# A second layout of x and an earlier row norm chain in layer 0, and another home for the gathered rows of the expert pairs

## The chip, the cores and the metric

The program runs on one core of one Trainium2 chip. TensorE (PE), VectorE (DVE), ScalarE (ACT) and GpSimd (POOL) each work through an instruction stream of their own, in order. SyncE (SP) issues most of the DMAs. The metric is the device time of one execution in microseconds (us), as the median of several runs. All arithmetic is in float32; many matmuls take operands split in a high and a low part (dtype float32r), three products to one.

## The reference

Two layers of an encoder on 512 tokens of width 1024:

```python
for l in range(DEPTH):                       # DEPTH = 2
    h = rmsnorm(x, attn_norm_g[l])
    x = x + hybrid_mixer(h, ...)             # h @ W_in (1024 x 2464), 16 attention heads, @ W_out
    h = rmsnorm(x, ffn_norm_g[l])
    x = x + expert_choice_ffn(h, ...)        # 16 experts, each takes its 64 best tokens
return rmsnorm(x, final_norm_g)

# expert_choice_ffn, for each expert e:
gate, idx = top_k(affinity[:, e], 64)
xe = h[idx]                                  # 64 x 1024
y  = (silu(xe @ w_gate[e]) * (xe @ w_up[e])) @ w_down[e]     # 1024 x 1408, 1024 x 1408, 1408 x 1024
out[idx] += y * gate
```

The rotary angles of the attention heads come from `positions`. The weights of the experts are some 277 MB for each layer; everything else is small beside that.

## The kernel before, in words

**Projection.** `attention` computes h @ W_in with the tokens along the matmul's columns (feature-major): `xh` and `xl` hold the high and the low part of x transposed and multiplied by the norm's gain, 8 row blocks k of 128 features by 512 tokens. The norm's factor per token is applied later: `row_norms` (L350) squares and sums x's rows on ACT (L354) and a power on POOL (L178) gives `rstd`, which `spread` (L360, PE at L364) turns into a row `rb`. The columns of W_in come in chunks. `split(i)` makes a chunk's weights into a high part (ACT, L332) and the rest (DVE, L333). PE then does 24 matmuls for a chunk (L733: 8 blocks k, three products). `spread` stands in PE's order behind the second chunk.

**x transposed.** `turn_x(t)` (L336) has PE transpose 8 blocks of 128 tokens (L342), DVE multiply them out of PSUM by the gain (`gx`, L346), ACT make the high part (L347) and DVE the rest (L348). `heat` (L368) puts matmuls on the identity in between, `START` says how many. This runs in both layers.

**Angles.** In layer 0 `make_angles` computes the rotary angles by some 45 small DVE instructions on 128x128 tiles (L212 to L231), pumped out ahead of the first chunk's matmuls; their sines go to ACT (L241), and `make_tables` (L246) spreads them by PE behind the third chunk.

**Experts.** They are worked through in 8 pairs. A pair takes 24 weight loads of 1408 KB: 8 row blocks of w_gate, 8 of w_up, 8 of w_down. `load` (L153) issues each on SP, into the buffer that `extra` names: `SEQ` for the first 16 loads of a layer, after that the list `again` round and round, 14 buffers. `x0` to `x11` are tiles of the expert pool, `s0` to `s2` of the ring that also holds W_in. A load can be issued when PE has done the matmuls on what lay in its buffer. The gathered rows of a pair's 128 tokens (indirect DMA from `xrow_d`, L1162, scaled on ACT, L1163) have buffer x0, which the first load of the layer has used. `turn_rows` (L1165) transposes them for PE. For the first pair the rows' first half is made by PE from x itself (`fill`, L1136), the second half comes from the gather.

**What sets the order.** Each engine's order is fixed when the program is built: a recording layer puts instructions in an order by its own priorities, except where `keep_in_program_order` pins one. A buffer of a pool is handed out again when its last reader is done.

**End of layer 0.** `put` (L1266) adds the last pair's results: for 6 of the 8 half blocks of x, PE has already put x itself into PSUM, and the sum is copied back (L1281) by ACT or DVE as `END_ON` says; the other two are added by DVE (L1279).

Of the kernel before, what the change touches and what calls it, by code (L numbers as in the profile page):

```python
# [11 lines left out]
F32 = mybir.dt.float32  # L12
# [119 lines left out]
def body(ctx, tc, x_in, pos, w_in, w_uq, w_ukv, w_out, w_gate, w_up, w_down, gatt, gfin, params, consts, band, sel, out):  # L132
# [53 lines left out]
    def make_angles(pool):  # L186
# [9 lines left out]
        for t in range(NT):  # L196
            nc.sync.dma_start(pi[32 * t : 32 * t + 32], pos[:, t * P : (t + 1) * P].to_broadcast([32, P]))
# [60 lines left out]
    def attention(l, ap, wk, op):  # L258
# [19 lines left out]
        xh = op.tile([P, KD, S], F32R, tag="big", name="xh")  # L278
        xl = [wk.tile([P, 4, S], F32R, tag="st", bufs=4, name=nm("xl")) for _ in range(2)]
# [19 lines left out]
        def fetch():  # L299
            if len(loaded) < len(plan):  # L300
# [13 lines left out]
        steps, sines = make_angles(wk) if l == 0 else (iter(()), None)  # L314
        nc.sync.dma_start(pg, params[l])
# [7 lines left out]
        def split(i):  # L323
# [13 lines left out]
        def turn_x(t):  # L337

            for h in range(2):
                pt = bank()  # L340
                for k in range(4):
                    nc.tensor.transpose(pt[:, k * P : (k + 1) * P], x[:, t, (h * 4 + k) * P : (h * 4 + k + 1) * P], ident)  # L342
                gx = wk.tile([P, S], F32, tag="P", bufs=PB, name=nm("gx")).rearrange("p (k s) -> p k s", k=4)
                g = gcol[:, l, h * 4 : h * 4 + 4].unsqueeze(2).to_broadcast([P, 4, P])
                hv = xh[:, h * 4 : h * 4 + 4, t * P : (t + 1) * P]
                nc.vector.tensor_tensor(gx, pt.rearrange("p (k s) -> p k s", k=4), g, op=ALU.mult)  # L346
                nc.scalar.copy(hv, gx)  # L347
# [1048 lines left out]
```

## Time and profile before

| what | us |
|---|---|
| median of 3 runs | 1937.29 (1937.24 to 1938.94) |
| the profiled execution, its own time | 1935.57 |
| its span | 1933.8 |
| PE busy | 1729.4 (89%) |
| DVE busy | 709.3 (37%) |
| ACT busy | 429.0 (22%) |
| bytes moved by DMA | 647.75 MB, mean 335 GB/s |

The span is the time from the first to the last instruction; 1.8 us of the execution's own time lie around it. A busy share of 89% for PE is a mean over stages with different limits, so it doesn't yet say what bounds the kernel. The chain of waits has DMA on 51% of the span and PE on 35%.

### The profile page before, as it was taken

Reading aid. Unit: us, or ns where it says so; the run is one execution under the profiler, and the core shown is the slowest. Engines: PE = TensorE matmul, PEld = TensorE weight load, DVE = VectorE, ACT = ScalarE, POOL = GpSimd, SP = SyncE. Lnnn points to the kernel's source line nnn. Section 1 sums busy time; section 2 is a strip of 40 time slices with the busy share of each in tenths; the row PEclk is TensorE's granted clock in tenths of the full one; section 3 lists DMA queues with packets and bytes.
Section 4 is the critical chain, followed back from the end, with each engine's and each line's share of the span. In section 5 each row is a group of like instructions: output and inputs, shape, how many; then the busy total and the mean of one; then the engine's idle time right before and its main releaser. Section 6 shows DMA issues by size and latency. Waiting matters only on the chain.

```text
span 1933.8 us, 22166 instructions
## 1 busy us (share of the span) xinstructions
PE 1729.4 (89%) x8838; PEld 888.7 (46%) x8838; DVE 709.3 (37%) x1481; ACT 429.0 (22%) x883; POOL 205.6 (11%) x232
## 2 busy tenths in 40 slices
PE   7999999999887888878889999989998888888786
PEld 6786676444332333323377856754443333323223
DVE  6877866211211112111178698551221112111112
ACT  4337952101000100000043489311100100001001
POOL 1314421000000000000013253110000000000000
PEclk9999999999999999999999999999999999999999
DMA  6765648899999999999938735689999999999996
GB/s 223 205 186 85 163 151 337 352 423 425 425 424 424 424 425 425 425 423 425 403 116 262 158 82 126 227 318 418 424 425 424 424 425 424 424 424 425 425 425 252
DMA packets 102758, 647.75 MB, mean 335 GB/s; under 512 B 11040, under 2 KB 28192, under 8 KB 53504
## 3 DMA queue, kind: packets, MB, share of 16 engines
q1 hardware_dynamic: 88336, 606.34, 77.9%
q0 software_dynamic: 12256, 36.07, 7.9%
q10 hardware_dynamic: 2064, 3.93, 0.6%
q8 instruction: 69, 1.13, 0.2%
q14 instruction: 33, 0.27, 0.0%
HBM read 617.60 MB, written 27.39 MB: 334 GB/s over the span
## 4 chain that ended last, share of the span: by engine, by line
DMA 51%; PE 35%; DVE 9%; ACT 3%; issue 1%; POOL 1%; SPq 0%; DVEq 0%; ACTq 0%; POOLq 0%
DMA xslot<-in_w_up_dram 12%; DMA xslot<-in_w_gate_dram 11%; DMA xslot<-in_w_down_dram 10%; PE ps L1215 7%; PE ps L733 6%; DMA slot<-in_w_up_dram 6%; DMA slot<-in_w_gate_dram 6%; DMA slot<-in_w_down_dram 6%; PE ps L834 4%; PE ps L1255 4%; PE ps L742 2%; PE ps L651 2%; PE ps L634 2%; DVE sm L583 1%; PE ps L494 1%
## 5 line engine op out<-in xcount | busy, mean ns | idle before, releaser
L1215 PE MATMUL ps<-xslot,xe 128*64 128x506 f32 (+1 forms) x2400 | 511.0, 566 | 80.1 <-DMA xslot<-in_w_up_dram 57.4
L1215 PEld LDWEIGHTS ps<-xslot,xe 128*64 128x64 f32 x2400 | 162.0, 137 | 410.7 <-issue 260.2
L1255 PE MATMUL ps<-xslot,hx 128*64 128x512 f32 (+3 forms) x1392 | 252.6, 507 | 35.6 <-DMA xslot<-in_w_down_dram 31.0
L1234 DVE TENSOR_TENSOR hx<-ps,hx 128x506 f32<-128x506 f32 (+1 forms) x48 | 43.5, 970 | 453.4 <-PE ps L1215 453.4
L1255 PEld LDWEIGHTS ps<-xslot,hx 128*64 128x64 f32 x1392 | 92.8, 137 | 186.1 <-issue 119.4
L1182 ACT ACTIVATE hx<-ps,gates 128x512 fp32r<-128x512 f32 x32 | 20.3, 684 | 676.2 <-PE ps L1255 676.2
L1215 PE MATMUL ps<-slot,xe 128*64 128x506 f32 (+1 forms) x648 | 140.4, 568 | 21.0 <-DMA slot<-in_w_up_dram 15.1
L1183 DVE SCALAR_TENSOR_TENSOR hx<-ps,gates,hx 128x512 fp32r<-128x512 f32 x32 | 22.5, 746 | 366.2 <-ACT hx L1182 366.2
L733 PE MATMUL ps<-xh,w 128*128 128x512 f32 (+1 forms) x448 | 146.0, 409 | 12.1 <-ACT xh L347 12.1
L1193 DVE TENSOR_TENSOR x<-ps,x 128x512 f32<-128x512 f32 x112 | 69.5, 683 | 172.5 <-PE ps L1191 172.5
L590 ACT ACTIVATE P<-ps,sm 128x512 f32<-128x512 f32 x168 | 116.6, 704 | 32.0 <-DVE sm L583 30.8
L1162 POOL DMA_INDIRECT xslot<-xrow_d,slots x16 | 15.3, 959 | 961.2 <-DVE oh L1155 942.2
L1163 ACT ACTIVATE xslot<-xslot,slots 128x1024 f32<-128x1024 f32 x16 | 18.4, 1148 | 442.9 <-DMA xslot<-xrow_d,slots 442.9
L733 PEld LDWEIGHTS ps<-xh,w 128*128 128x128 f32 (+1 forms) x448 | 85.7, 192 | 36.0 <-ACT xh L347 13.2
L1215 PEld LDWEIGHTS ps<-slot,xe 128*64 128x64 f32 x648 | 44.0, 137 | 110.8 <-issue 71.0
L733 PE MATMUL ps<-xl,w 128*128 128x512 f32 (+1 forms) x224 | 85.7, 393 | 0.0
L583 DVE TENSOR_REDUCE sm<-ps 128x1 f32<-128x512 f32 x120 | 78.7, 679 | 5.8 <-PE ps L568 4.8
L1255 PE MATMUL ps<-slot,hx 128*64 128x512 f32 (+3 forms) x400 | 71.7, 498 | 9.2 <-DMA slot<-in_w_down_dram 8.4
L634 PE MATMUL ps<-ident,P 128*128 128x128 f32 x512 | 77.8, 275 | 1.2 <-ACT P L590 1.1
L642 ACT COPY pt<-ps 128x512 f32<-128x512 f32 x118 | 68.9, 605 | 26.0 <-PE ps L634 25.8
L634 PEld LDWEIGHTS ps<-ident,P 128*128 128x128 f32 x512 | 62.6, 141 | 24.5 <-ACT P L590 7.0
L333 DVE TENSOR_TENSOR w<-slot,w 128x1024 fp32r<-128x1024 f32 (+4 forms) x46 | 53.8, 1171 | 30.2 <-ACT w L332 27.2
(280 smaller groups left out, 2119.9 us busy)
## 6 DMA issues: line engine op xcount, KB each, us to landing
xslot<-in_w_gate_dram SPq DMA_DIRECT2D x100, 1408.0 KB, 27.1
xslot<-in_w_up_dram SPq DMA_DIRECT2D x100, 1408.0 KB, 28.0
xslot<-in_w_down_dram SPq DMA_DIRECT2D x100, 1408.0 KB, 27.0
slot<-in_w_gate_dram SPq DMA_DIRECT2D x28, 1408.0 KB, 27.1
slot<-in_w_down_dram SPq DMA_DIRECT2D x28, 1408.0 KB, 27.0
slot<-in_w_up_dram SPq DMA_DIRECT2D x26, 1408.0 KB, 28.3
slot<-in_w_in_dram SPq DMA_DIRECT2D x8, 1536.0 KB, 7.3
st<-bst_d POOLq DMA_DIRECT2D x40, 256.0 KB, 4.4
```

Of the source, the lines that this page charges most:

```text
L333: nc.vector.tensor_tensor(w[:, 1, :, o : o + m], src, w[:, 0, :, o : o + m].bitcast(F32), op=ALU.subtract)
L583: nc.vector.tensor_reduce(mn, ps, axis=AX.X, op=ALU.min)
L590: nc.scalar.activation(e, ps, AF.Exp, bias=mn, scale=-1.0, accum_out=lcol)
L634: nc.tensor.transpose(b[:, kc * P : (kc + 1) * P], e[:, kc * P : (kc + 1) * P], ident)
L642: nc.scalar.copy(dv, bv)
L651: nc.tensor.matmul(o[64 * i : 64 * i + 64], heads[2 * m + i][4][:, kc, :], pts[i][:, kc, :], start=(kc == 0), stop=(kc == NT - 1))
L733: nc.tensor.matmul(b[:m], w[:, passes[j][0], k, :m], passes[j][1](k), start=(n == 0), stop=(n == 3 * KD - 1))
L834: nc.tensor.matmul(blocks[t][1 + h], o, w[h], start=(i == 0), stop=(i == 3 * KD - 1))
L1193: nc.vector.tensor_tensor(xv, b, xv, op=ALU.add)
L1215: tc.keep_in_program_order(nc.tensor.matmul(b[64 * i : 64 * i + 64, : qn * NJ], xe[:, k, 64 * i : 64 * i + 64], ws[i][:, q0 * NJ : (q0 + q ...
L1234: nc.vector.tensor_tensor(hv, u[:, : qn * NJ].rearrange("p (q j) -> p q j", j=NJ), hv, op=ALU.mult)
L1255: tc.keep_in_program_order(nc.tensor.matmul(bs[h][64 * i : 64 * i + 64, e % 512 : e % 512 + z - e], hT[:, j, 64 * i : 64 * i + 64], ws[i][ ...
```

## The change

In layer 0 a second copy of x, transposed (`x_t`), is loaded where x was, and the parts are made from it without PE; x itself is loaded later. The positions come ready for one DMA. The angles are pumped out ahead of the row norm, and all of `START` stands ahead of the first chunk. In layer 1 the transposes follow each other without a break, and the low parts are pinned behind all of them. In the experts, the first pair's rows are fetched as half rows into a third buffer of the tag `oh`; the other pairs' rows have x7, the buffer of the tenth load, in place of x0, and the second pair's are fetched later (`ROWS_AT`). `END_ON` is all ACT.

```diff
-START = [[6, 0, 2, 6, 4], [2, 0, 0, 4, 2]]
+START = [18, 2]
+ROWS_IN = 7
+ROWS_AT = 2
-END_ON = 'avavav'
+END_ON = 'aaaaaa'
...
-        for t in range(NT):
-            nc.sync.dma_start(pi[32 * t : 32 * t + 32], pos[:, t * P : (t + 1) * P].to_broadcast([32, P]))
+        nc.sync.dma_start(pi, pos)
...
+        xs = [wk.tile([P, 4, S], F32, tag="st", bufs=4, name=nm("xs")) for _ in range(2 if l == 0 else 0)]
...
                     if l == 0 and not loaded and a == 0:
-                        for t in range(NT):
-                            tc.keep_in_program_order(nc.sync.dma_start(x[:, t, :], x_in[t * P : (t + 1) * P, :]))
+                        for k in range(0, KD, 2):
+                            src = x_t[k * P : (k + 2) * P, :].rearrange("(k p) s -> p k s", p=P)
+                            tc.keep_in_program_order(nc.sync.dma_start(xs[k // 4][:, k % 4 : k % 4 + 2, :], src))
...
         steps, sines = make_angles(wk) if l == 0 else (iter(()), None)
+        if l == 0:
+            for t in range(NT):
+                tc.keep_in_program_order(nc.sync.dma_start(x[:, t, :], x_in[t * P : (t + 1) * P, :]))
...
-                nc.vector.tensor_tensor(w[:, 1, :, o : o + m], src, w[:, 0, :, o : o + m].bitcast(F32), op=ALU.subtract)
+                rest = lambda o=o, m=m, src=src: nc.vector.tensor_tensor(w[:, 1, :, o : o + m], src, w[:, 0, :, o : o + m].bitcast(F32), op=ALU.subtract)
+                if lower is None:
+                    rest()
+                else:
+                    lower.append(lambda rest=rest: tc.keep_in_program_order(rest()))
...
-                nc.vector.tensor_tensor(xl[h][:, :, t * P : (t + 1) * P], gx, hv.bitcast(F32), op=ALU.subtract)
+            return lambda: tc.keep_in_program_order(nc.vector.tensor_tensor(xl[h][:, :, t * P : (t + 1) * P], gx, hv.bitcast(F32), op=ALU.subtract))
+
+        def part_x(k):
+
+            g, xv = gcol[:, l, k : k + 1], xs[k // 4][:, k % 4, :]
+            nc.scalar.activation(xh[:, k, :], xv, AF.Copy, scale=g)
+            nc.vector.scalar_tensor_tensor(xl[k // 4][:, k % 4, :], xv, g, xh[:, k, :].bitcast(F32), op0=ALU.mult, op1=ALU.subtract)
...
-        if l > 0:
-            ready = split(0)
-        for t in range(NT):
-            heat(START[l][t])
-            turn_x(t)
+        heat(START[l])
         if l == 0:
             ready = split(0)
-        heat(START[l][NT])
+            for k in range(KD):
+                part_x(k)
+            pump(100)
+        else:
+            ready = split(0, lower := [])
+            rest = {(t, h): turn_x(t, h) for t in range(NT) for h in range(2)}
+            for fn in lower + [rest[t, h] for h in range(2) for t in range(NT)]:
+                fn()
         rstd = row_norms()
...
-        pump(100)
...
-                again = [q for q in SEQ if q not in (0, "hx")]
+                again = [q for q in SEQ if q not in (ROWS_IN, "hx")]
...
-            slots = fw.tile([P, 144], F32, tag="slots", bufs=1, name=nm("slots"))
-            info = slots[:, 0:128].rearrange("p (t g i) -> p t g i", t=NT, g=8)
+            slots = fw.tile([P, 16], F32, tag="slots", bufs=1, name=nm("slots"))
+            info = pg[:, 0:128].rearrange("p (t g i) -> p t g i", t=NT, g=8)
...
-                v = xslot(0)[:, :D]
-                nc.gpsimd.indirect_dma_start(v, None, xrow_d[l][:, :], bass.IndirectOffsetOnAxis(token[:, p : p + 1], 0))
+                if p > 0:
+                    v, src = xslot(ROWS_IN)[:, :D], xrow_d[l][:, :]
+                else:
+                    v, src = fw.tile([P, S], F32R, tag="oh", bufs=3, name=nm("rows")).bitcast(F32), xrow_d[l].rearrange("t (h d) -> (t h) d", h=2)
+                nc.gpsimd.indirect_dma_start(v, None, src, bass.IndirectOffsetOnAxis(token[:, p : p + 1], 0))
...
                         if w is w_gate and k == MARK_AT and p < 7:
                             ohs[p + 1] = marks(p + 1)
-                            rows = fetch_rows(p + 1)
+                            if p > 0:
+                                rows = fetch_rows(p + 1)
+                        if w is w_up and k == ROWS_AT and p == 0:
+                            rows = fetch_rows(1)
```

VectorE at the start of layer 0, before (`gx`, `xl`: parts of x; `w`: the second chunk's rest; `tabw`: angles):

```order
L346 TENSOR_TENSOR gx_283<-ps_278,gcol 128x512
L346 TENSOR_TENSOR gx_292<-ps_287,gcol 128x512
L213 CAST tabw_192<-tabw_192 128x128
L348 TENSOR_TENSOR xl_177<-gx_283,xh 128x4x128
L348 TENSOR_TENSOR xl_178<-gx_292,xh 128x4x128
L214 TENSOR_SCALAR tabw_192<-tabw_192,cn 128x128
L333 TENSOR_TENSOR w_380<-slot_179,w_380 128x1024
L215 TENSOR_SCALAR tabw_192<-tabw_192 128x128
```

VectorE at the same place now, from its first weights on:

```order
L339 TENSOR_TENSOR w_229<-slot_181,w_229 128x1024
L363 SCALAR_TENSOR_TENSOR xl_179<-xs_177,gcol,xh 128x512 x4
L363 SCALAR_TENSOR_TENSOR xl_180<-xs_178,gcol,xh 128x512 x4
L339 TENSOR_TENSOR w_324<-slot_181,w_324 128x1024
L214 CAST tabw_194<-tabw_194 128x128
L215 TENSOR_SCALAR tabw_194<-tabw_194,cn 128x128
L216 TENSOR_SCALAR tabw_194<-tabw_194 128x128
```

Eight products out of PSUM and the instructions around them are gone; two angle steps have moved behind the second chunk's rest.

VectorE a little later in layer 0 now, where the row norm's `v` stands, which before was the fifth of its rows:

```order
L210 TENSOR_SCALAR tabw_195<-tabw_195 128x128
L211 TENSOR_TENSOR tabw_195<-tabw_195 128x128
L372 TENSOR_SCALAR v_293<-ss_284 128x4
L231 COPY tabw_195<-tabw_195 128x128
L232 TENSOR_SCALAR tabw_195<-tabw_195 128x128
```

The step that leads to `rstd` has moved behind most of the angles.

VectorE at the start of layer 1, before, from the last sums of x on:

```order
L1279 TENSOR_TENSOR x<-ps_5766,x 128x512
L1279 TENSOR_TENSOR x<-ps_5770,x 128x512
L346 TENSOR_TENSOR gx_5883<-ps_5878,gcol 128x512
L346 TENSOR_TENSOR gx_5892<-ps_5887,gcol 128x512
L346 TENSOR_TENSOR gx_5901<-ps_5896,gcol 128x512
L348 TENSOR_TENSOR xl_5858<-gx_5883,xh 128x4x128
L346 TENSOR_TENSOR gx_5910<-ps_5905,gcol 128x512
L348 TENSOR_TENSOR xl_5859<-gx_5892,xh 128x4x128
L333 TENSOR_TENSOR w_5872<-slot_5860,w_5872 128x1024
L348 TENSOR_TENSOR xl_5858<-gx_5901,xh 128x4x128
L348 TENSOR_TENSOR xl_5859<-gx_5910,xh 128x4x128
L346 TENSOR_TENSOR gx_5919<-ps_5914,gcol 128x512
```

The same stretch now (five of the eight `gx`, then the rest of the first weights):

```order
L355 TENSOR_TENSOR gx_5850<-ps_5845,gcol 128x512
L355 TENSOR_TENSOR gx_5858<-ps_5853,gcol 128x512
L355 TENSOR_TENSOR gx_5866<-ps_5861,gcol 128x512
L355 TENSOR_TENSOR gx_5874<-ps_5869,gcol 128x512
L355 TENSOR_TENSOR gx_5882<-ps_5877,gcol 128x512
L339 TENSOR_TENSOR w_5819<-slot_5804,w_5819 128x1024
L357 TENSOR_TENSOR xl_5802<-gx_5826,xh 128x4x128
L357 TENSOR_TENSOR xl_5802<-gx_5842,xh 128x4x128
```

All eight `gx` stand ahead of every `xl` and of the weights' rest.

## Rows read from the trace of the kernel before

**Rows 1.** Windows: from:to, length, busy of each engine (count), PEclk, DMA share, GB/s.

```profile
8.00:10.00 2.00, 2.00 (x13) 2.00 (x12) 0.00 (x0) 1.54 (x4) 0.00 (x0) 1.00 1.03 418
...
21.70:26.70 5.00, 5.00 (x12) 3.94 (x13) 4.79 (x16) 0.54 (x1) 0.00 (x0) 0.50 0.80 265
...
41.20:125.00 83.80, 83.80 (x360) 63.40 (x359) 73.46 (x117) 26.60 (x41) 27.26 (x21) 1.00 0.69 210
...
337.00:345.60 8.60, 7.53 (x49) 4.40 (x46) 2.33 (x8) 0.00 (x0) 1.09 (x1) 1.00 0.23 98
...
357.00:435.00 78.00, 77.28 (x413) 31.67 (x413) 14.33 (x26) 6.32 (x7) 1.90 (x2) 1.00 1.01 423
...
1290.90:1297.70 6.80, 5.73 (x26) 2.70 (x26) 2.11 (x7) 0.00 (x0) 1.08 (x1) 0.75 0.22 63
```

**Rows 2.** Chain that ended last: start, length, what; one chunk, one steady load.

```profile
35.82 5.57 PE ps L733 x24
...
435.04 27.17 DMA xslot<-in_w_down_dram
```

**Rows 3.** Timeline, start of layer 0: start, length, instruction, count, idle before and releaser.

```profile
6.90 1.06 ACT L354 ACTIVATE junk<-x 128x1024 f32<-128x1024 f32 x1 [0.17 <-DMA x<-in_x_dram]
...
6.92 3.28 PE L342 MATMUL ps<-ident,x 128*128 128x128 f32 x16 [2.48 <-DMA x<-in_x_dram]
...
12.38 1.04 POOL L178 TENSOR_TENSOR r<-v,mhalf 128x4 f32<-128x4 f32 x1 [9.02 <-DVE v L357]
...
12.70 1.04 PE L342 MATMUL ps<-ident,x 128*128 128x128 f32 x8
...
13.30 1.05 ACT L332 CAST w<-slot 128x1024 fp32r<-128x1024 f32 x1 [1.21 <-DMA slot<-in_w_in_dram]
...
21.70 6.25 PE L733 MATMUL ps<-xh,w 128*128 128x512 f32 x16 [7.00 <-ACT xh L347]
...
23.08 1.22 DVE L333 TENSOR_TENSOR w<-slot,w 128x1024 fp32r<-128x1024 f32 x1
...
31.90 0.29 DVE L210 TENSOR_TENSOR tabw<-tabw 128x128 f32<-128x128 f32 x1
...
35.22 0.60 PE L364 MATMUL ps<-ident,r 128*128 128x128 f32 x4
```

**Rows 4.** Timeline, first expert pair of layer 0: weight loads, first steps, gather.

```profile
327.14 0.43 SPq L155 DMA_DIRECT2D slot<-in_w_up_dram  x1
...
335.82 2.58 PE L1215 MATMUL ps<-xslot,xe 128*64 128x506 f32 x12 [0.38 <-DVE xe L1139]
...
342.91 2.58 PE L1215 MATMUL ps<-xslot,xe 128*64 128x506 f32 x12
...
343.87 1.09 POOL L1162 DMA_INDIRECT xslot<-xrow_d,slots  x1 [9.52 <-PE ps L1150]
...
345.54 3.93 SPq L155 DMA_DIRECT2D xslot<-in_w_down_dram  x2
...
351.39 0.65 PE L1170 MATMUL ps<-ident,xslot 128*128 128x128 f32 x4
```

**Rows 5.** DMA issues at 327.14 and 378.35: count, KB, us to landing.

```profile
slot<-in_w_up_dram SPq DMA_DIRECT2D x1, 1408.0 KB, 13.8
...
xslot<-in_w_gate_dram SPq DMA_DIRECT2D x1, 1408.0 KB, 14.9
```

**Rows 6.** Timeline, start of layer 1.

```profile
969.61 1.87 DVE L346 TENSOR_TENSOR gx<-ps,gcol 128x512 f32<-128x512 f32 x3
...
975.79 1.88 DVE L346 TENSOR_TENSOR gx<-ps,gcol 128x512 f32<-128x512 f32 x3
...
978.37 1.96 PE L733 MATMUL ps<-xh,w 128*128 128x512 f32 x5 [4.70 <-ACT xh L347]
...
980.11 0.62 ACT L347 CAST xh<-gx 128x512 fp32r<-128x512 f32 x1 [1.79 <-DVE gx L346]
...
991.60 0.60 PE L364 MATMUL ps<-ident,r 128*128 128x128 f32 x4
```

More of the change, by code (lines that the diff above doesn't have):

```diff
@@ L131, in body @@
 @with_exitstack
-def body(ctx, tc, x_in, pos, w_in, w_uq, w_ukv, w_out, w_gate, w_up, w_down, gatt, gfin, params, consts, band, sel, out):
+def body(ctx, tc, x_in, x_t, pos, w_in, w_uq, w_ukv, w_out, w_gate, w_up, w_down, gatt, gfin, params, consts, band, sel, out):
     nc = tc.nc
@@ L321, in attention, with split @@
         fetch()
-        def split(i):
+        def split(i, lower=None):
             gi, cols, ks = chunks[i]
@@ L332, in split, with turn_x @@
                 nc.scalar.copy(w[:, 0, :, o : o + m], src)
-                nc.vector.tensor_tensor(w[:, 1, :, o : o + m], src, w[:, 0, :, o : o + m].bitcast(F32), op=ALU.subtract)
+                rest = lambda o=o, m=m, src=src: nc.vector.tensor_tensor(w[:, 1, :, o : o + m], src, w[:, 0, :, o : o + m].bitcast(F32), op=ALU.subtract)
[3 more added lines that the diff above has]
+                    lower.append(lambda rest=rest: tc.keep_in_program_order(rest()))
                 o += m
             return w, o
[L337 to L347, printed above, removed]
-                nc.vector.tensor_tensor(xl[h][:, :, t * P : (t + 1) * P], gx, hv.bitcast(F32), op=ALU.subtract)
+        def turn_x(t, h):
+            pt = bank()
+            for k in range(4):
+                nc.tensor.transpose(pt[:, k * P : (k + 1) * P], x[:, t, (h * 4 + k) * P : (h * 4 + k + 1) * P], ident)
+            gx = wk.tile([P, S], F32, tag="P", bufs=PB, name=nm("gx")).rearrange("p (k s) -> p k s", k=4)
+            g = gcol[:, l, h * 4 : h * 4 + 4].unsqueeze(2).to_broadcast([P, 4, P])
+            hv = xh[:, h * 4 : h * 4 + 4, t * P : (t + 1) * P]
+            nc.vector.tensor_tensor(gx, pt.rearrange("p (k s) -> p k s", k=4), g, op=ALU.mult)
+            nc.scalar.copy(hv, gx)
+            return lambda: tc.keep_in_program_order(nc.vector.tensor_tensor(xl[h][:, :, t * P : (t + 1) * P], gx, hv.bitcast(F32), op=ALU.subtract))
[3 more added lines that the diff above has]
+            nc.vector.scalar_tensor_tensor(xl[k // 4][:, k % 4, :], xv, g, xh[:, k, :].bitcast(F32), op0=ALU.mult, op1=ALU.subtract)
         def row_norms():
@@ L1098, in body @@
             state["extra"] = extra
-            slots = fw.tile([P, 144], F32, tag="slots", bufs=1, name=nm("slots"))
-            info = slots[:, 0:128].rearrange("p (t g i) -> p t g i", t=NT, g=8)
-            token, scales = slots[:, 128:136].bitcast(I32), slots[:, 136:144]
+            slots = fw.tile([P, 16], F32, tag="slots", bufs=1, name=nm("slots"))
+            info = pg[:, 0:128].rearrange("p (t g i) -> p t g i", t=NT, g=8)
+            token, scales = slots[:, 0:8].bitcast(I32), slots[:, 8:16]
             nc.gpsimd.tensor_copy(info[:, :, :, 0:2], a_all.rearrange("p t (g i) -> p t g i", i=2))
@@ L1222, in body @@
                             if k == HALF_AT:
-                                turn_rows(rows, xe, 4)
+                                turn_rows(rows, xe, 4, 4)
                         if w is w_gate and k in SCATTER_AT and pending is not None:
@@ L1347, in shape_constants @@
     return consts, band, np.tile(sel.reshape(32, 6 * P), (4, 1))
-_INS = ["x", "positions", "w_in", "mla_w_uq", "mla_w_ukv", "w_out", "w_gate", "w_up", "w_down", "gatt", "gfin", "params", "consts", "band", "sel"]
+_INS = ["x", "x_t", "positions", "w_in", "mla_w_uq", "mla_w_ukv", "w_out", "w_gate", "w_up", "w_down", "gatt", "gfin", "params", "consts", "band", "sel"]
 def lay_out(inputs):
@@ L1359, in lay_out @@
     got["x"] = a["x"].reshape(S, D)
-    got["positions"] = a["positions"].reshape(1, S)
+    got["x_t"] = np.ascontiguousarray(got["x"].T)
+    got["positions"] = np.repeat(a["positions"].reshape(NT, P), 32, axis=0)
     got["gatt"] = np.ascontiguousarray(a["attn_norm_g"].reshape(L, KD, P).transpose(2, 0, 1))
```

13 lines of the change are left out of this document (8 added, 5 removed).

## The prediction

> **What bounds the kernel now.** I read four views, in this order. First the windows by stage: the reader is to see that the limit changes from stage to stage. In layer 0's attention PE is busy 83.80 of 83.80 us while the DMA engines are at 0.69: PE bounds. From 357 us on the DMA share is 1.01 at 423 GB/s: the stream of expert weights bounds, although PE is nearly full as well (77.28 of 78) [rows 1]. Second, the chain of waits: DMA holds 51% of it, and a steady load takes 27.17 us there, while one chunk of the projection is 5.57 us of PE [rows 2]. So the time is the start of the full stream, plus bytes over rate, plus the tail. Whatever makes the attention of a layer end earlier carries through in full, and so does whatever fills the stream earlier.
>
> Third, the timeline where layer 0 starts: before its first weight-chunk matmul PE waits 7.00 us for `xh`, and then runs at half the clock: 16 matmuls in 6.25 us, where 16 of a full-speed chunk are 16/24 x 5.57 = 3.7 [rows 2, 3]; the windows say 0.50 there [rows 1]. `spread` stands at 35.22 [rows 3].
>
> Fourth, the first expert pair. The 16th load is issued at 327.14 and lands 13.8 us later, at 340.9. The 17th is issued only at 345.54, 0.05 us after the second gate step has ended (342.91 + 2.58 = 345.49) [rows 4, 5]: the first step's buffer x0 has gone to the gathered rows, so the first load that comes round again takes the second step's. In between DMA is at 0.23, and at 0.22 at the same place of layer 1 [rows 1]. That is a hole in the stream that bounds.
>
> **Layer 0's start: -9.8 us.** x's second copy stands in the queue where x stood, so its first piece should come about when x came, at 6.9 [rows 3]. ACT makes eight parts `xh` at 0.62 each [rows 6], from 6.9 to about 12; the first chunk's last blocks end about 16 (16 matmuls at full clock, 3.7), the second chunk 5.6 later at 21.7. PE's transposes and their eight `gx` are gone, and the half-clock stretch with them, as PE no longer idles for 7 us. If nothing else held, PE would be at `spread` at 21.7 in place of 35.22: -13.5.
>
> But the row norm holds it. DVE now has the second chunk's rest, the angles, and only then `v`. Before, the stretch from that rest (23.08) to the angle step at 31.90 + 0.29 took 9.1 us [rows 3]. Now the rest can follow ACT's cast of the second piece, which ends at 13.30 + 1.05 = 14.35 [rows 3]; two angle steps of 0.3 each have moved behind it. So the angles reach that step at 14.4 + 9.1 + 0.6 = 24.1, `v` is done at 24.3, POOL's power (1.04) at 25.4, and `spread` starts at 25.4: 35.22 - 25.4 = 9.8 earlier. Before, that same `r` was ready at 13.4, far ahead of PE; it takes the lead of the chain only now. PE idles some 3.7 us.
>
> Does x itself come in time for the squares? It follows the second piece (13.3); 2 MB at 418 GB/s [rows 1] are 5 us, with latency 20; the last square (1.06, [rows 3]) ends near 22, 2 us before `v`. That is a narrow margin. Bounds: -13.5 if the norm never holds PE, and -7 if the second copy or x lands some 3 us late.
>
> **Layer 0's experts: -3.4.** The rows of later pairs have x7 now, so x0 serves the 17th load, which waits for the first gate step (335.82 + 2.58 = 338.40) in place of the second (345.49) [rows 4]. From there each load is issued where its predecessor was: the stream is one load ahead, 1408 KB (1.44 MB) at 423 GB/s [rows 1], 3.4 us. The bytes are the same, so what is won is that much of the hole. Cover: at 378.35 a load takes 14.9 us to land [rows 5], of which the transfer alone is 3.4, so loads stand in a queue by then and a step of PE that is late by less than that doesn't reopen the hole. The half gather of the first pair has its own buffer; its rows are used at 351.39 [rows 4] as before.
>
> The second pair's gather moves behind x7's last use, to `w_up`'s third step; its scaling on ACT (128x1024, as long as a square, about 1.1 [rows 3]) stands ahead of the first pair's SILUs there and may delay them by its length, which the queued loads hide. It must be early enough for the second pair, which begins more than 60 us later. Bounds: 0, if PE is the limit up to 435 (77.28 of 78 leaves it 0.7 us), and -5 if the lighter gather frees the queues as well. I take 3.4: the DMA share of 1.01 is the nearer row.
>
> **The layer boundary: -4.2.** Eight `gx` now follow each other: from about 969.4 on, just ahead of where three stood together before (969.61), at 0.62 each (1.87 for three) [rows 6], to 974.4, where before the last three ended at 977.7. The six copies, all on ACT now, I estimate to end near 969.5 (six of the length of an `xh`, 3.7 us, from 965.8); then eight `xh` at 0.62 and two casts of weights at 1.05 [rows 3, 6] bring it to 976.9, where the last `xh` ended at 980.73 [rows 6]. DVE then does the weights' rest (1.22 [rows 3]) and eight `xl` at 0.63, to 980.6. The first chunk ends near 981.5, the second at 987.3, so `spread` stands at 987.4 against 991.60 [rows 6]. Bounds: -1.5, if the six copies queue on ACT behind each other and delay `xh`; -5, if PE's wait of 4.70 [rows 6] goes altogether.
>
> **Layer 1's experts: -3.4**, by the same step; the hole at 1290.9 looks the same (0.22), only that PE's clock is 0.75 in it [rows 1], so that up to 1 us more could come back if PE doesn't stop. Bounds 0 and -5.
>
> **Nothing** for the positions in one DMA, the smaller `slots`, and the token's product: they stand beside long waits of their engines.
>
> **Sum.** -9.8 - 3.4 - 4.2 - 3.4 = -20.8 against the profiled execution's own 1935.57 gives 1914.8. The median of the runs shown is 1937.29, 1.7 above it: forecast 1916.5. The likeliest case's own range, from its four terms' bounds taken as independent, is some 4 us to either side.
>
> **The rivals.**
>
> *The clock falls in the new gaps.* PE now idles about 3.7 us before `spread`, and in layer 1 between the transposes and the first chunk. After 7.00 us of waiting, sixteen matmuls took 6.25 in place of 3.7, so 2.5 us is what such a fall costs [rows 2, 3]. One fall gives 1919, two 1921.5. For it: in layer 1 only two matmuls of `heat` are left, and the rest of PE's work ahead of the first chunk is transposes. Against it: the new gaps are half as long as that of 7.00.
> A rule of the Trainium skill bears on this ("TensorE: Matmul & The Clock Gate", Part 1: The HAM clock gate): throttled is the default, and activity releases it. By it the gap in front of `spread`, and a start of layer 1 with less heat, would be where the fall comes; the trace agrees as far as [rows 1, 3] go, with 0.50 behind the idle 7.00.
> The same page (Part 4: PE-mode transpose) has it that transposes don't count as work there, which would speak against layer 1's new start, where they are nearly all that stands ahead of the chunk; the trace doesn't settle it: transposes went from 3.28/16 = 0.21 us each to 1.04/8 = 0.13 [rows 3], but with `heat`'s plain matmuls between them.
>
> *The lead of one load does not carry.* If PE bounds the pair up to 435 (77.28 of 78 busy [rows 1]), both expert terms are given back: 1914.8 + 6.8 + 1.7 = 1923.3. Against it: the share of 1.01 beside it, and loads that wait in the queue for 14.9 us [rows 5].
>
> *The row norm does not hold PE.* Were DVE's angles through sooner than before, the full 13.5 would come: 1912.8. Against it: DVE's 9.1 us are mostly its own instructions.
>
> *The second copy lands late.* Its pieces arrive as runs of one row's 2 KB; with 3 us more for ACT's parts, the second piece of weights and all behind it shift: 1919.5.
>
> *Slower than before.* The same mechanism at a larger price: were the second copy's 2 MB to take 30 us more than x's, the sum of -20.8 would become +9.2: 1946.5. It decides from the point where the copy takes 20.8 us longer than the 5 us reckoned with: 2.1 MB in 26 us, some 80 GB/s. The rows of this start show 418 [rows 1], and the first piece of x came at 6.9 [rows 3].
>
> **How the numbers follow.** Forecast 0.67, a fall of the clock 0.13, no lead 0.10, the full 13.5 0.05, a late copy 0.03, slower 0.02. The range of 8 in 10: from 1910.5 (the full 13.5 with some more from layer 1) to 1926 (the lead lost and one fall of the clock). A measurement of this kernel can tell about 0.2%, 3.9 us, from no change. All cases but the last lie at least 14 us below the time before: faster 0.96; within 0.2% 0.02; slower 0.02.
>
> **What would show it.** In the new profile the first transposes of `r` start at about 25.4 and wait for POOL, with 3 to 4 us of idle PE ahead; if they wait for nothing, the norm never held. The granted clock behind that gap and at layer 1's start decides the second rival. The 17th load's issue stands within 0.1 us of the first gate step's end, and the DMA share in the hole rises from 0.23; if the issue moves but the share from 357 falls below 1, the lead didn't carry. In layer 1 the distance from the last sum of x to `spread` shrinks by 4 us. The prediction is wrong if `v` is found waiting for ACT's squares, or if first matmuls wait for x's second copy past 9 us.

## The result and the profile after

The changed kernel takes 1915.43 us in the median of 4 runs (1914.84 to 1920.75), the kernel before beside it 1937.65: a ratio of 0.9892, with an interval of 0.9879 to 0.9905. Forecast were 1916.5 us; faster was the likeliest sign. Its profiled execution has a span of 1913.7 us, 20.1 below the 1933.8 of before; the sum of the forecast was 20.8. In the chain of waits DMA has gone from 51% to 48% and PE from 35% to 37%.

Seven points of the trace cut the span into the stages of the forecast. The last product is ACT's first multiplication by the gates in a layer's last pair (L1182, now L1205). A negative number is a gain over the stage of before; "again" is a second profile of the same changed kernel, which the experiments below come to.

| point | at, before | at, after | stage up to it: forecast | stage: after | stage: again |
|---|---|---|---|---|---|
| `spread`, layer 0 | 35.22 | 25.63 | -9.8 | -9.6 | -9.8 |
| first gate step, layer 0 | 335.82 | 326.36 | 0 | +0.1 | +1.1 |
| last product, layer 0 | 963.72 | 951.25 | -3.4 | -3.0 | -4.0 |
| `spread`, layer 1 | 991.60 | 975.84 | -4.2 | -3.3 | -3.0 |
| first gate step, layer 1 | 1286.34 | 1271.16 | 0 | +0.6 | +1.9 |
| last product, layer 1 | 1915.06 | 1894.95 | -3.4 | -4.9 | -4.8 |
| end of the span | 1933.8 | 1913.7 | 0 | 0.0 | 0.0 |
| sum | | | -20.8 | -20.1 | -18.7 |

The timeline of the changed kernel's start answers to [rows 3]; the columns are those.

```profile
1.52 6.92 PE L387 MATMUL ps<-ident 128*128 128x128 f32 x36 [1.52 <-POOL ident masks.py:199]
...
8.58 4.10 ACT L362 ACTIVATE xh<-xs,gcol 128x512 fp32r<-128x512 f32 x6 [0.43 <-DMA xs<-in_x_t_dram]
...
12.12 2.96 PE L750 MATMUL ps<-xh,w 128*128 128x512 f32 x10 [0.30 <-ACT xh L362]
...
14.81 1.23 DVE L339 TENSOR_TENSOR w<-slot,w 128x1024 fp32r<-128x1024 f32 x1 [1.29 <-ACT w L338]
...
21.58 0.18 ACT L369 ACTIVATION_READ_ACCUMULATOR junk<-x 128x1 f32 x1
...
24.28 0.16 DVE L372 TENSOR_SCALAR v<-ss 128x4 f32<-128x4 f32 x1
24.53 1.04 POOL L180 TENSOR_TENSOR r<-v,mhalf 128x4 f32<-128x4 f32 x1 [21.16 <-DVE v L372]
25.63 0.65 PE L379 MATMUL ps<-ident,r 128*128 128x128 f32 x4 [3.10 <-POOL r L180]
```

Read it from the bottom. `spread` waits 3.10 us, for POOL's power; this starts when `v` ends; and `v` had been free to run since the last square ended, at 21.58 + 0.18 = 21.76. It ran at 24.28 because DVE had the angles ahead of it, and a last rest of weights among them. The title calls this chain earlier; in time it is not: `r` is ready at 24.53 + 1.04 = 25.57 here, and was at 12.38 + 1.04 = 13.42 before [rows 3]. What comes earlier is `spread`, which now waits for it. x's second copy brings PE to work at once: ACT's parts wait 0.43 us for it and end at 12.7.

The timeline of the first pair of layer 0 in the changed kernel answers to [rows 4].

```profile
326.36 2.58 PE L1238 MATMUL ps<-xslot,xe 128*64 128x506 f32 x12 [0.38 <-DVE xe L1156]
...
328.99 11.02 SPq L157 DMA_DIRECT2D xslot<-in_w_down_dram  x3
...
333.45 2.58 PE L1238 MATMUL ps<-xslot,xe 128*64 128x506 f32 x12
...
341.93 0.66 PE L1193 MATMUL ps<-ident,rows 128*128 128x128 f32 x4
```

The 17th load goes out at 328.99, 0.05 us after the first gate step (326.36 + 2.58 = 328.94). The windows of the changed kernel over the same stretches, counted from the first gate step, answer to [rows 1]; the last two are layer 1's hole and the first 16 matmuls of layer 1. A PEclk of 1.00 is the full clock and 0.50 half of it; what lies between is a mean over a window in which it changed.

```profile
327.50:336.10 8.60, 7.53 (x49) 4.36 (x46) 2.34 (x8) 0.00 (x0) 1.10 (x1) 1.00 0.64 231
347.50:425.50 78.00, 76.15 (x407) 31.18 (x408) 14.34 (x26) 6.34 (x7) 1.91 (x2) 1.00 1.01 421
1275.70:1282.50 6.80, 5.73 (x37) 3.39 (x38) 2.34 (x8) 0.00 (x0) 1.09 (x1) 1.00 0.73 252
963.30:968.30 5.00, 4.96 (x16) 4.00 (x17) 5.00 (x9) 4.94 (x9) 0.00 (x0) 0.71 0.00 0
```

The DMA share in the holes has risen from 0.23 to 0.64 and from 0.22 to 0.73, and the stream behind stays at 1.01. The last row is the blemish: layer 1's first chunk runs at a clock of 0.71.

The timeline of layer 1's start answers to [rows 6].

```profile
956.21 3.66 PE L351 MATMUL ps<-ident,x 128*128 128x128 f32 x32
956.85 4.88 DVE L355 TENSOR_TENSOR gx<-ps,gcol 128x512 f32<-128x512 f32 x8
...
961.11 2.70 ACT L356 CAST xh<-gx 128x512 fp32r<-128x512 f32 x5
...
963.34 5.25 PE L750 MATMUL ps<-xh,w 128*128 128x512 f32 x16 [3.47 <-ACT xh L356]
...
975.84 0.60 PE L379 MATMUL ps<-ident,r 128*128 128x128 f32 x4
```

Eight `gx` stand in one piece, 4.88 us. PE waits 3.47 us in place of 4.70, and then takes 5.25 us for 16 matmuls that cost 3.7 at full speed.

### The profile page after: what moved, and what is told of

The parts are those of the page before. It is cut to its first block, busy times and chain, and to the rows that moved or that the text cites. A ratio compares the mean times of both kernels' runs of the same rounds, so it can differ in the third digit from the quotient of the medians.

```text
span 1913.7 us, 22070 instructions
## 1 busy us (share of the span) xinstructions
PE 1714.9 (90%) x8794; PEld 882.3 (46%) x8794; DVE 703.5 (37%) x1470; ACT 429.9 (22%) x886; POOL 205.5 (11%) x232
## 4 chain that ended last, share of the span: by engine, by line
DMA 48%; PE 37%; DVE 8%; ACT 3%; issue 1%; POOL 1%; SPq 0%; DVEq 0%; ACTq 0%; POOLq 0%
DMA xslot<-in_w_gate_dram 13%; DMA xslot<-in_w_down_dram 13%; DMA xslot<-in_w_up_dram 9%; PE ps L1238 8%; DMA slot<-in_w_up_dram 7%; PE ps L750 6%; PE ps L1281 5%; PE ps L851 5%; DMA slot<-in_w_gate_dram 3%; PE ps L759 2%; PE ps L669 2%; PE ps L652 2%; DMA slot<-in_w_down_dram 1%; PE ps L512 1%; DVE sm L601 1%
## 5 line engine op out<-in xcount | busy, mean ns | idle before, releaser
L1238 PE MATMUL ps<-xslot,xe 128*64 128x506 f32 (+1 forms) x2400 | 505.8, 562 | 80.7 <-DMA xslot<-in_w_up_dram 57.8
L1205 ACT ACTIVATE hx<-ps,gates 128x512 fp32r<-128x512 f32 x32 | 20.3, 684 | 657.2 <-PE ps L1281 657.2
L1238 PE MATMUL ps<-slot,xe 128*64 128x506 f32 (+1 forms) x648 | 138.5, 561 | 19.6 <-DMA slot<-in_w_up_dram 14.4
L750 PEld LDWEIGHTS ps<-xh,w 128*128 128x128 f32 (+1 forms) x448 | 84.1, 189 | 29.2 <-ACT xh L356 3.7
L759 PE MATMUL ps<-w,xh 128*128 128x320 f32 (+1 forms) x256 | 62.2, 326 | 2.3 <-DVE w L339 2.3
```

The lines of the kernel that those rows point to most:

```text
L750: nc.tensor.matmul(b[:m], w[:, passes[j][0], k, :m], passes[j][1](k), start=(n == 0), stop=(n == 3 * KD - 1))
L759: nc.tensor.matmul(acc[t][:, :m], xs, w[:, c, kk, :], start=(k == 0 and j == 0), stop=(k == KD - 1 and j == 2))
L1238: tc.keep_in_program_order(nc.tensor.matmul(b[64 * i : 64 * i + 64, : qn * NJ], xe[:, k, 64 * i : 64 * i + 64], ws[i][:, q0 * NJ : (q0 + q ...
```

## The experiments

Single runs of one and the same kernel lie up to 7 us apart (those of before, from 1935.07 to 1942.26 on one chip), and the ratios' intervals are some 0.0014, or 2.7 us, to either side. What is smaller is read from the stages of the profiles, which hold chance of their own, as will be seen.

**The later pairs' rows in x0 again.**

```diff
-ROWS_IN = 7
+ROWS_IN = 0
```

> The changed kernel, but the later pairs' rows have x0 again; the first pair's half rows and the later fetch stay. Theory (the stream is one load ahead because the 17th load waits for the first gate step and not the second, and everything behind it is bound by the stream): the 17th load is issued at the second gate step's end again, and both layers give back what they gained, 3.0 us in layer 0 and 4.9 in layer 1 by the changed kernel's trace, so 1915.4 + 7.9 = about 1923. Rival (the gain is from the lighter gather, or PE bounds there): within 1 us of 1915.4.

Measured: 1924.91 us (ratio 0.9934, 0.992 to 0.9948), 9.5 above the changed kernel; by the profiles the expert stages are 628.2 and 627.9 us long, against 624.9 and 623.8 in the changed kernel and 627.9 and 628.7 before. So the expert stages' whole gain is gone with one number, 7.4 us, and the lighter gather, which this kernel keeps, is worth nothing measurable. Its timeline shows the 17th load behind the second gate step:

```profile
325.77 2.58 PE L1238 MATMUL ps<-xslot,xe 128*64 128x506 f32 x12 [0.38 <-DVE xe L1156]
332.86 4.28 PE L1238 MATMUL ps<-xslot,xe 128*64 128x506 f32 x12
```

```profile
337.18 3.93 SPq L157 DMA_DIRECT2D xslot<-in_w_down_dram  x2
```

The second step took 4.28 us here and 2.58 in the changed kernel: the clock fell in this execution. The rest of the difference, 2 us, lies in layer 1's start and attention, which this edit doesn't touch. There, too, it is the clock: behind the same wait the first 16 matmuls of layer 1 took 6.57 us in place of 5.25, and in the 10 us ahead of layer 1's first gate step the clock was 0.55 in place of 0.90.

```profile
966.10 6.57 PE L750 MATMUL ps<-xh,w 128*128 128x512 f32 x16 [3.47 <-ACT xh L356]
```

**The rows in x2.**

```diff
-ROWS_IN = 7
+ROWS_IN = 2
```

> The changed kernel, but the later pairs' rows have x2, the buffer of the fifth load, in place of x7, that of the tenth. Theory (the lead of one load stays only if loads stand in a queue by the time the left-out buffer's turn comes): the 21st load, issued at 346.0 in the changed kernel with 8.2 us to landing (about 7 is what a load alone takes), then moves 4 us back, and with only some 1.4 us of backlog the queue runs dry for about 2.5 us in each layer: 1920 to 1921. Rival (any buffer after the first does, the lead is won once the 17th load is early): 1915.4.

Measured: 1919.47 us (0.991, 0.9894 to 0.9925), 4.0 above; span 1918.3, 4.6 above. The stages are 627.6 and 627.5 long: each has lost about 3 of its gain. In layer 0 the second gate step ran at a fallen clock (3.96 us); in layer 1 it did not, and there the loss shows alone. From 20 to 25 us behind layer 1's first gate step a second hole opens; the first row is the changed kernel's, the second that with x2:

```profile
1291.16:1296.16 5.00, 5.00 (x30) 2.31 (x31) 1.16 (x5) 0.00 (x0) 0.00 (x0) 1.00 0.99 410
1292.13:1297.13 5.00, 5.00 (x30) 2.32 (x31) 1.16 (x5) 0.00 (x0) 0.97 (x1) 1.00 0.68 238
```

The rival is out: an early 17th load alone wins next to nothing that lasts. The stream keeps its lead only if a queue of loads has built up before the left-out buffer's turn. With x2 the turn comes at the 21st load, which goes out 23.6 us behind the first gate step, as with x0 (19.6 with x7). With x7 it comes at the 26th, which goes out at 35.4, also as with x0; but by then loads stand in the queue, and the DMA engines don't run dry.

Layer 1's start was 1.2 us shorter in this profile than in the changed kernel's, which hides part of the loss. The order there is the same and so is the wait, but the clock stayed at 1.00:

```profile
965.59 4.00 PE L750 MATMUL ps<-xh,w 128*128 128x512 f32 x16 [3.46 <-ACT xh L356]
```

(The run with x0 lies 5.4 us above this one; of the 4.8 between their two profiles, 3.9 are layer 1's start and attention, where the clock differed.)

**The copies at the end of layer 0 shared again.**

```diff
-END_ON = 'aaaaaa'
+END_ON = 'avavav'
```

> The changed kernel with the last pair's six copies of layer 0 shared between ACT and DVE again. Theory: DVE has three copies (1.9 us) ahead of its own two sums and the eight gx, which are the first thing that the layer's start waits for, so gx begins up to 1.9 us later, less what PE's own 16 matmuls of the sums allow; the chunk follows: plus 1 to 1.9 us, 1916.5 to 1917.3. Rival (ACT's six copies in a row were as late as DVE's): no change.

Measured: 1918.39 us (1914.87 to 1921.79); the median alone tells nothing against 1915.43. The stage from the last product to `spread` is 2.7 us shorter than before, where the changed kernel had 3.3 in one profile and 3.0 in the other. `gx` starts 0.3 us later behind the last product, and the first 16 matmuls took 5.53 us, as in the changed kernel's second profile: so the copies are worth 0.3, and what is over that is the clock. This is under what I expected, since DVE's three copies partly ran while PE still made the last sums. The profile shows something else, at the start: PE waited 1.83 us at `spread`, and in the 6 us behind it the clock was 0.73.

```profile
25.19 0.93 PE L379 MATMUL ps<-ident,r 128*128 128x128 f32 x4 [1.83 <-POOL r L180]
```

```profile
25.60:31.60 6.00, 6.00 (x22) 4.20 (x21) 2.48 (x4) 5.11 (x12) 0.00 (x0) 0.73 1.07 367
```

**Layer 1's start as before.**

```diff
-END_ON = 'aaaaaa'
+END_ON = 'avavav'
...
-            return lambda: tc.keep_in_program_order(nc.vector.tensor_tensor(xl[h][:, :, t * P : (t + 1) * P], gx, hv.bitcast(F32), op=ALU.subtract))
+            nc.vector.tensor_tensor(xl[h][:, :, t * P : (t + 1) * P], gx, hv.bitcast(F32), op=ALU.subtract)
...
-            ready = split(0, lower := [])
-            rest = {(t, h): turn_x(t, h) for t in range(NT) for h in range(2)}
-            for fn in lower + [rest[t, h] for h in range(2) for t in range(NT)]:
-                fn()
+            ready = split(0)
+            for t in range(NT):
+                heat([0, 0, 0, 4][t])
+                for h in range(2):
+                    turn_x(t, h)
+            heat(2)
```

> The changed kernel with layer 1's start as before: copies shared, low parts among the gx, heat in three places. Theory: the 3.3 us by which the distance from the last pair's products to spread shrank come back, less the 0.6 that the attention behind lost: 1918.1 to 1918.7; with the run on the copies alone this gives the order's own share. Rival (the attention of layer 1 absorbs the shift): 1916 or less.

Measured: 1920.51 us (0.9907, 0.9891 to 0.9922); the stage from the last product to `spread` is as long as before, to 0.1 us. So, with a fall of the clock in all of them, the order of `gx` and low parts is worth 2.6 us of the stage (2.7 with the copies shared, 0.1 here) and the copies 0.3. The profile has two falls of the clock that the edit can't have caused: one in the second gate step of layer 0, and one at layer 0's start, where the two kernels are the same:

```profile
25.39 1.11 PE L379 MATMUL ps<-ident,r 128*128 128x128 f32 x4 [3.12 <-POOL r L180]
```

```profile
25.60:31.60 6.00, 6.00 (x17) 4.20 (x17) 2.49 (x4) 5.29 (x13) 0.00 (x0) 0.51 1.07 365
```

A wait of 3.12 us, and half the clock for 6 us; the changed kernel waited 3.10 and kept its full clock (28 matmuls in 5.97 us of its window from 25.60 to 31.60). The fall cost 2.4 us. The length of the wait alone does not decide it.

**`v` in the middle of the angles.** `v` and the angles' step L228 are pinned in this order.

```diff
-            yield V.tensor_add(f, f, ah)
+            yield tc.keep_in_program_order(V.tensor_add(f, f, ah))
...
-            nc.vector.tensor_scalar(v, ss, 1.0 / D, 1e-6, op0=ALU.mult, op1=ALU.add)
+            op_ = nc.vector.tensor_scalar(v, ss, 1.0 / D, 1e-6, op0=ALU.mult, op1=ALU.add)
+            if l == 0:
+                tc.keep_in_program_order(op_)
...
-            pump(100)
+            pump(22)
...
         rstd = row_norms()
+        pump(100)
```

> The changed kernel, but v of the row norm stands in DVE's order where ACT's squares are done (21.8 by the changed kernel's trace), in the middle of the angles, in place of behind the first wrap. Theory (the chain squares, v, POOL, spread holds PE, not PE's own work): v at 21.9, r at 23.1, spread at 23.2 in place of 25.63, so 2.4 us earlier, PE's wait 0.7 in place of 3.1; the tables come behind the third chunk at 29.3, when the sines (ready at 29.2 in the changed kernel) are just there. With so short a wait the clock cannot fall there either, which it did in the run with the shared copies and in that with layer 1's old start. Median 1912 to 1913.5. Rival (DVE's angles are what the attention waits for next): spread moves, but the tables don't, and the time stays at 1915.

Measured: 1916.63 us (0.9895, 0.988 to 0.991), no gain. `spread` came at 23.84 and so 1.8 us earlier, and waits for nothing any more, but the tables came only 0.7 earlier (31.68 in the changed kernel, the last row):

```profile
23.84 0.60 PE L381 MATMUL ps<-ident,r 128*128 128x128 f32 x4
...
29.67 1.25 ACT L242 ACTIVATE wide_w<-tabw 32x128 f32<-32x128 f32 x4
30.97 5.42 PE L251 MATMUL ps<-wide_w,sl 128*128 128x512 f32 x12 [0.96 <-ACT wide_w L242]
```

```profile
31.68 5.31 PE L251 MATMUL ps<-wide_w,sl 128*128 128x512 f32 x12
```

PE waits at the tables for the sines in place of waiting at `spread`. The rival was right in the main: the sines stand close behind, and 0.7 us is less than the time can tell.

**`v` ahead of all angles.**

```diff
-            pump(100)
...
         rstd = row_norms()
+        pump(100)
```

> The changed kernel, but the row norm is recorded ahead of all angles, so v stands in DVE's order in front of the first of them. Theory (x's squares, not DVE, are then the last thing: v can't be ready before 21.8): spread at 23.2 as in the run with v in the middle, but the angles start only at 22 and end some 6 us later than in the changed kernel (31 to 32), the sines at 35, and PE waits for the tables behind the third chunk: the tables start at about 35 in place of 31.7, so 2 to 4 us slower than the changed kernel, 1917.5 to 1919.5. Rival (only spread matters): as with v in the middle, 1912 to 1913.

Measured: 1927.38 us (0.9949, 0.9935 to 0.9962), 12 us above the changed kernel; expected were 2 to 4. The sign is that of the theory, the price much larger: 8.8 us are lost ahead of layer 0's first gate step. Some 3 more lie in layer 1's start and attention, which this edit doesn't touch and where the clock was lower in this profile (the first 16 matmuls took 6.80 us). `spread` is as early as in the run before, 23.56, but:

```profile
21.56 0.17 DVE L372 TENSOR_SCALAR v<-ss 128x4 f32<-128x4 f32 x1 [1.52 <-ACT junk L369]
...
34.81 0.23 DVE L231 COPY tabw<-tabw 128x128 f32<-128x128 f32 x1
35.11 1.28 ACT L242 ACT_TABLE_LOAD   x1 [3.76 <-DVE tabw L231]
36.41 2.54 ACT L242 ACTIVATE wide_w<-tabw 32x128 f32<-32x128 f32 x8
39.00 1.22 PE L251 MATMUL ps<-wide_w,sl 128*128 128x512 f32 x1 [9.26 <-ACT wide_w L242]
```

The angles don't only start later, they are also mixed with the projection's products (L433) and weights, since DVE's order was laid out again around the earlier `rb`. PE waits 9.26 us, and then the tables take 7.39 us at a fallen clock where they took 5.31.

**Matmuls on the identity in layer 1's wait.**

```diff
+HEAT_END = 12
...
             for fn in lower + [rest[t, h] for h in range(2) for t in range(NT)]:
                 fn()
+            heat(HEAT_END)
```

> The changed kernel with 12 matmuls on the identity behind layer 1's transposes, in PE's wait of 3.47 us for the parts. Theory (the clock falls because PE idles there; 16 matmuls took 5.25 us at 0.71 where 3.7 is full speed): the chunk runs at full clock, spread of layer 1 comes 1.5 us sooner after the last pair's products, 1914. Rival (the first chunk is held by the parts xh and xl, not by the clock): no change.

Measured: 1915.96 us (0.9897, 0.9882 to 0.9913), not to be told from the changed kernel by its time; by the profile the stage from the last product to `spread` is 4.6 us shorter than before, 1.3 better than the changed kernel's.

```profile
960.22 2.84 PE L388 MATMUL ps<-ident 128*128 128x128 f32 x24
963.85 3.94 PE L752 MATMUL ps<-xh,w 128*128 128x512 f32 x16 [0.79 <-ACT xh L357]
```

The 16 matmuls take 3.94 us in place of 5.25, at a clock of 1.00. (The twelve matmuls on the identity, in float32, stand as 24 rows.) So it was the clock and not the parts; the profile with the rows in x2 says the same without any added work, with 4.00 us and a stage 4.5 shorter than before.

**Both together.** The edits of the last run and of `v` in the middle.

> The changed kernel with v in the middle of the angles and the 12 matmuls on the identity at layer 1's start. Theory: both gains add, 2.4 + 1.5, 1911 to 1912. Rival: a gain at layer 0's start is lost in the attention: 1914.

Measured: 1915.31 us (0.9888, 0.9873 to 0.9903), as the changed kernel. Layer 1's stage has the 4.6 again and `spread` of layer 0 came at 23.24, but the clock fell in the second gate step of both layers (3.78 and 4.21 us in place of 2.58) and took part of it back, and the tables waited 1.04 us for the sines again. The expected 1911 to 1912 weren't reached.

**The first pair's marks one step later**, on top of both.

```diff
-FIRST_MARKS = 0
+FIRST_MARKS = 1
```

> The run with v in the middle and heat behind layer 1's transposes, and with the first pair's marks behind the second gate step in place of the first, in both layers. Theory (the 18th load waits for the second gate step, and this waits for the marks): that step starts 2.5 us earlier behind the first, the 18th load moves from 9.7 to 7.2 us behind the first step's start, the later ones by some 0.8, the marks' gather still lands before its transposes: 0.8 to 1 us in each layer, so the expert stages of both layers get 0.8 to 1 us shorter, 1913.5 in all. Rival (the gather comes too late, and the transposes of the rows wait): 2 us longer in each layer.

Measured: 1917.11 us (0.9898, 0.9884 to 0.9912). The 18th load did move, from 9.7 to 7.1 us behind the first gate step, but the next ones did not (13.3 in layer 1, as in the changed kernel), and layer 1's expert stage is 624.3 long, no shorter than the changed kernel's 623.8. The theory's 0.8 us did not come. (In layer 0 the third gate step took 4.22 us, at a window's clock of 0.60.)

**Layer 0's start alone.** The edits of layer 1's start as before and of the rows in x0, together.

> Layer 0's start as in the changed kernel (second copy of x, angles ahead of the norm), and the other parts taken back: shared copies and layer 1's old start, the later pairs' rows in x0. Theory (the parts are worth what their stages show and add up): the first gate step of layer 0 comes 9.5 us earlier than before, and each later stage is as long as before, within the 1.7 us by which a stage differs between executions when the clock falls in the first pair: 1937.3 - 9.5 = 1927.8. Rival (the stream hides part of an earlier start): 1930 or more.

Measured: 1927.45 us (0.9947, 0.9934 to 0.996). The first gate step comes 10.1 us earlier, and of that 8.2 are left at the end (span 1925.6): the stages in between are 0.3 to 0.7 us longer than before, each for itself within what executions differ by. The start is worth by itself what it is worth in the changed kernel: 1937.0 - 9.5 = 1927.5. The rival is out.

**No matmuls ahead of the first chunk.**

```diff
-START = [18, 2]
+START = [0, 2]
```

> The changed kernel without the 18 matmuls on the identity ahead of the first chunk. Theory (the row norm's chain sets spread, and PE has 3.1 us to spare in front of it): the first chunk runs at half the clock, for some 5 us as it did before, and loses about 2.5 us, PE's wait shrinks from 3.1 to about 0.6, and spread stays at 25.6; no change of the time. Rival (PE's own work sets spread): spread at 28, plus 2.5.

Measured: 1921.76 us (0.9921, 0.9908 to 0.9935), 6.3 above; `spread` at 27.55, against both expectations in part.

```profile
9.36 7.03 PE L750 MATMUL ps<-xh,w 128*128 128x512 f32 x14 [0.20 <-ACT xh L362]
...
18.29 0.93 ACT L338 CAST w<-slot 128x512 fp32r<-128x512 f32 x2 [3.61 <-PE ps L750]
...
26.20 0.16 DVE L372 TENSOR_SCALAR v<-ss 128x4 f32<-128x4 f32 x1
...
27.55 1.11 PE L379 MATMUL ps<-ident,r 128*128 128x128 f32 x4 [3.76 <-POOL r L180]
```

PE still waits for the norm, even longer (3.76), so its own work isn't what sets `spread`. But the norm is late as well: in this kernel's order ACT casts the third chunk's weights ahead of the squares, and that cast waits 3.61 us for the first chunk to leave its buffer. The clock was 0.60 in the window from 25 to 30 and 0.72 in that from 30 to 35. The edit moved the order with it, and so doesn't test what it was meant to.

**The changed kernel once more.**

> The changed kernel once more, unaltered, for a second profile of it. Theory (the falls of the clock behind spread's wait, 1 to 2.4 us, and in the first pair's second gate step, 1.7 us, belong to an execution and not to a kernel): the time's median within 2 us of 1915.4, its single times 4 to 6 us apart, and the two profiles of one and the same kernel differ from each other in at least one of these places. Rival (each kernel has its falls in fixed places): stage by stage the second profile agrees with the first within 0.3 us.

Measured: 1916.71 us (1916.16 to 1920.28; 0.9903, 0.9889 to 0.9917), 19.0 below the kernel before beside it (1935.68), where the first comparison had 22.2. Its profile makes the test that the last edit missed. Here the first chunk was slow by itself:

```profile
11.90 4.32 PE L750 MATMUL ps<-xh,w 128*128 128x512 f32 x10 [0.27 <-ACT xh L362]
...
25.38 0.65 PE L379 MATMUL ps<-ident,r 128*128 128x128 f32 x4 [1.76 <-POOL r L180]
```

The ten matmuls took 4.32 us in place of 2.96, the wait shrank from 3.10 to 1.76, and `spread` stayed where it was. The order is the same here, and PE's slack is real. This first chunk is no exception: of the eight profiles in which layer 0's start has the changed kernel's order, six had it slow, with waits of 1.59 to 1.97 us at `spread`, and two had it at full clock, with 3.10 and 3.12; `spread` stood between 25.19 and 25.63 in all of them. The two profiles agree in layer 1's expert stage to 0.1 us and differ by 1.0 and 1.3 us in the two attentions: just ahead of layer 0's first gate step (323 to 327) the clock was 0.61 in this one, and in the 10 us ahead of layer 1's it was 0.55, against 0.90 in the first. In `spread`'s wait and in the first pair neither profile had a fall, so the difference that was expected there didn't come; it came in the first chunk and ahead of the gate steps. That the falls at `spread` and in the first pair belong to an execution, too, rests on the runs above: up to the end of layer 0 the orders of all engines are the same in the changed kernel and in those with the shared copies and with layer 1's old start.

## Why the prediction was right

*The start.* Every link was found where it was put: the second chunk's rest 14.81 (14.4), `v` 24.28, ending at 24.44 (24.3), `spread` 25.63 (25.4), the squares done 2.5 us before `v` (2). The row norm holds PE: shown by the profile taken once more, where PE lost 1.3 us and `spread` didn't move, and by `v` in the middle, where it did. The working had PE's own two chunks at full clock, done at 21.7; they ended at 22.3 and 22.5 in two profiles of this start and at 23.4 to 23.9 in six, and the wait for the norm hid it. What I had not seen is how little is behind `spread`: in the changed kernel the last sine is ready at 29.2 and the tables begin at 31.7, so that, by this trace, not more than some 2.5 us could be won at `spread` before PE waits for the sines. The full 13.5 us of the third rival would have met them first; `v` in the middle did so after 0.7 us, as the sines themselves moved back.

*The experts.* The term of 3.4 us for each layer was right in mechanism and in size, with one correction: "each load is issued where its predecessor was" holds from the 17th to the 25th load only. The 26th goes out where it did with x0, and the lead lives on in the queue. The mean of the two profiles is 3.5 in layer 0. In layer 1 it was 4.9 and 4.8; the second gate step took 3.94 us before at the clock of 0.75 [rows 1], which was a fall in that execution (with x0 in the changed kernel the same step took 2.58, and the stage 627.9). Against that stage the gain is 627.9 - 623.8 = 4.1.

```profile
1293.71 3.94 PE L1215 MATMUL ps<-xslot,xe 128*64 128x506 f32 x12
```

What is over 3.4 of this is spread between executions. Fourteen stages of the profiles have x7, the first pair's marks as they are and no fall in the second gate step: they last 623.7 to 625.1 us, 624.4 in the mean. Two have x0 and no such fall, 627.9 each. The difference is 3.5. The cover was tested too: with x2 in place of x7 the lead is lost. The rival that PE bounds the pair is out, with PE at 76.15 of 78 and DMA at 1.01.

*The layer boundary.* The term of -4.2 was the one that failed: -3.3 and -3.0 were measured. The step that I had as "the first chunk ends near 981.5" took no fall of the clock into account, though [rows 6] had one (PE's 5 matmuls in 1.96 us). PE waits 3.47 us behind the transposes and then has 0.71 (0.66 in the other profile); with twelve identity matmuls in that wait the stage gives 4.6. So the rival of the falling clock came true here, at a price of 1.3 us in place of 2.5. But 1.3 is one draw of several: six profiles have the same order here and the same wait (the changed kernel's two, x2, x0, `v` in the middle, and no matmuls ahead of the first chunk). The 16 matmuls took 5.25, 5.53, 4.00, 6.57, 6.64 and 5.53 us in them, and the stage gave 3.3, 3.0, 4.5, 1.9, 1.9 and 3.0. The fall cost from nothing to 2.6 us, by the execution; that the term came within 1 us of its forecast is in part luck. The trace agrees with the rule of the Trainium skill that was cited for it ("TensorE: Matmul & The Clock Gate", Part 1): with work in the wait the clock stayed released, in all three profiles that had it. The profile with x2 shows that without it the clock needn't fall either. Whether transposes count as work is left open, since the added matmuls stood behind them and also closed the wait.

*The sum.* -20.8 was forecast, -20.1 and -18.7 came. The difference is the boundary's 1 us and attentions that lost 0.1 to 1.9 us, the more the lower the clock ahead of the gate steps, against layer 1's experts, which gave 1.5 more. These misses have opposite signs, so that the sums agree to 0.7 us is in part luck.

*The slower side.* x's second copy at a rate under 80 GB/s: the parts waited 0.43 us for it.

## What to carry to other kernels

Where a stream bounds, look for the load whose issue waits longest behind an empty queue, and ask which buffer's release it waits for: giving the gathered rows another home in a list of 14 was worth 7 us by the stages of the profiles, and the same edit five loads earlier only about 1.5. A wait at one place in an in-order queue is not won back by moving its releaser forward unless what stood behind it (here the sines) has slack as well. And when a part is priced to a microsecond, judge it by the length of its stage between two points of a trace, since whole runs of one kernel differ by more than that, and by several profiles, since a fall of the clock moved one and the same stage by up to 2.6 us.

## What the runs showed that I had not expected

After almost the same wait (3.10 and 3.12 us) with the same instructions on both sides, PE kept its clock at full in one execution and had half of it for 6 us in another; after 1.83 us in a third it was at 0.73. In the first pair's second gate step, behind a wait of 1.07 us, such a fall made 2.58 us into 4.28.

```profile
332.00 1.03 PE L1165 MATMUL ps<-pgf,oh 128*128 128x4 f32 x8 [1.07 <-DVE oh L1127]
```

(This is the wait in the changed kernel, where the step behind it took its 2.58.) At layer 1's start a wait of 3.5 us was followed by anything from the full clock to half of it. The length of a wait alone did not decide in any of these places, and such falls, of 1 to 2.6 us each, are the largest differences that I can name between profiles of equal stages.

The column of the granted clock doesn't show the start: the 36 matmuls on the identity at 1.52 took 0.19 us each in the mean (they start 0.21 apart at first and 0.11 from the 27th on), and 24 of the same kind at 960.22 in layer 1 took 0.12, but the windows around both read 1.00. At the start, durations tell the clock and the column doesn't.
